# New prices for the clocks that choose a kernel's order of issue

## The chip, the cores and the metric

The kernel runs on one core of a Trainium2 chip. What is measured is the time of one execution in microseconds (us) on the device. Engines are called as in the profile: PE is the tensor engine's matmul and PEld its weight load, DVE the vector engine, ACT the scalar engine, POOL GpSimd, SP the queue that issues the transfers.

## The reference

One layer of a backbone over 256 latent tokens with 256 context tokens before them, width 2048, all in float32. Cut to what matters:

```python
h_ctx = rmsnorm(ctx) * (1 + scale_c) + shift_c      # scale, shift: products of silu(c) with w_mod
h     = rmsnorm(x)   * (1 + scale)   + shift
p     = h @ w_in                                    # 11552 columns, for both streams
r, k, v = split(conv3x3(p[rkv]))                    # the RWKV branch: 16 heads of 64
S = S*diag(w_t) + (S a_t) b_t^T + v_t k_t^T;  y_t = S r_t   # over the tokens, forwards and backwards
o = chunked_gla(q, k, v, g)                         # the GLA branch: 4 heads, forwards and backwards
mixed = sigmoid(g_a) * (y_a @ w_a) + sigmoid(g_b) * (y_b @ w_b)
out   = rmsnorm(x + gate * (mixed @ w_out))
```

The context is scanned first, and its last states are the first states of the latent tokens.

## The kernel before

Every product with a large weight is "dense": weights come in chunks of 512 KB (tile `raw`), ACT rounds half a chunk to a high part `wH`, DVE subtracts to get the rest `wL`, and PE sums three products of the parts (`three`). Dense work fills four stages in turn: the modulation and the first products; phase A (about 165 to 600 us in the profile), the rest of the columns for both streams with the GLA branch beside them; phase B (about 600 to 1170 us), columns that only latent tokens need, with the RWKV branch beside them; phase C, the two branch projections and the output projection.

The RWKV branch goes by eight pairs of heads. For each pair `fe_track` makes features on all engines, `gg_track` multiplies them in chunks, `inv_track` inverts the triangles on POOL in 30 steps of two instructions (`tm`, then `M`) between copies on ACT (`Lin`) and 32-wide transposes on DVE and two sets of small products on PE (`pH`, `pZ`), and `sc_track` carries the states through 8 chunk steps. A chunk step is a chain: product `p` on PE, copy `R` on ACT, product `pU`, copies into `UV` on DVE and ACT, product `pSs`, `Sn` on DVE, copies into `UV`, and the next `p`. In each of these products PE works on a part of its array (128x64 or 64x64 instead of 128x128); `pgl` has 64x128, `pH` and `pZ` 32x32.

The order is not written by hand. The program is cut into tracks (generators that yield an instruction, a list for one engine, or a claim to a bank of PSUM). While the program is built, `Issue.run` keeps a rough clock for each engine and advances the track whose next instruction can start first; among those of the same engine within 40 ns of it, the lowest priority number wins, and dense products have the highest number, 99. So dense work is what PE gets while nothing small is ready by the clocks. Each engine then runs its instructions in that fixed order on the chip, and waits at any whose inputs are late. The clocks decide nothing else: no instruction is added or left out by them.

The prices are in `Op.__init__` (line 31): for PE a weight load, a stream of columns and how many passes; for the others an offset and so many ns per element. `Issue.emit` (line 146) moves the clocks on:

```python
for _ in range(n):
    self.load_at = max(self.load_at, self.stream_at, there) + ld
    self.stream_at = max(self.load_at, e + 2)
    e = self.stream_at + stream
```

`there` is the time at which the inputs are there. Small float32 products that lie in different corners of the array are priced as running side by side (`corners`). `warm` (line 135) says whether PE has its full clock by the planner's own count, and doubles PE's prices where not; `cooling` (line 139) then prefers dense work. Two more uses of the prices: after 1200 ns of small work a dense list is taken if it stands in the same 40 ns (`since`), and `pace` (line 1491) lets gate columns start by how much small work was priced so far (`small`).

Every recorded operation has line 303 in the profile, where `Eng` calls the engine, so tiles tell them apart.

Of the kernel before, what the change touches and what calls it, by code (L numbers as in the profile page):

```python
# [24 lines left out]
class Op:  # L25
    """An instruction that a track wants issued."""

    __slots__ = ("key", "name", "call", "out", "ins", "cost", "table", "acc", "pe")

    def __init__(self, key, name, call, out, ins, func, acc, psum):  # L30
        self.key, self.name, self.call, self.out, self.ins, self.acc = key, name, call, out, ins, acc
        self.table = None if func not in TABLES else TABLES[func]
        n = 1
        for s in out.shape[1:]:
            n *= s
        per = 0
        if name in ("activation", "tensor_scalar", "scalar_tensor_tensor") and n > 1:
            per = sum(1 for x in ins if len(x.shape) == 2 and x.shape[1] == 1)
        if key == "pe":
            m = 1  # L40
            for s in ins[0].shape[1:]:
                m *= s
            if name == "transpose":
                m = n = ins[0].shape[0]
            two = ins[0].dtype == F32 and name != "transpose"
            self.pe = (2 if two else 1, m / 1.2, max(n, 64 if m > 32 else 32) * (2 if two else 1) / 2.4,
                       two and m <= 64 and (Issue.box(ins[0])[0], Issue.box(out)[0], m),
                       n * (2 if two else 1) * ins[0].shape[0] / 128)
            c = self.pe[0] * max(self.pe[1:3])
        elif key == "act":  # L50
            c = (51 if psum else 94) + 0.833 * n + 93 * per
        elif key == "dve":
            if name == "tensor_reduce":
                n = 1
                for s in ins[0].shape[1:]:
                    n *= s
            fast = name in ("tensor_copy", "tensor_scalar") and not psum
            c = (6 if name == "memset" else 68) + n * (0.521 if fast else 1.042) + 61 * per
        elif key == "pool":
            c = 35 + 0.83 * n if name == "memset" else 110 + 3.36 * n if name == "tensor_copy" else 149 + (  # L60
                1.667 if any(q == 0 and k > 1 for x in ins for q, k in x.ap[1:]) else 2.096) * n
        else:
            c = max(475.0, out.shape[0] * n * 4 / 360.0)
        self.cost = c

# [4 lines left out]
class Claim:  # L70
    """A free bank of PSUM from a group, once what is to be multiplied is there."""
# [5 lines left out]
class Issue:  # L77
    """Chooses the order in which the program is issued.

    Every engine runs its instructions in the order of issue. The program is cut into tracks: generators that yield  # L80
    an instruction (or a list of them for one engine), a claim to a bank of PSUM, or a condition. Of all tracks the
    one whose next instruction can start first, by rough clocks of the engines, is advanced; among those of one
    engine that could start at about the same time the one with the lowest priority number.
    """
# [3 lines left out]
    TICK, COLUMNS = 10240 / 3, 3060  # L88

    def __init__(self, ps, groups):  # L90
# [9 lines left out]
        self.corners, self.ticks = [], {}  # L100

# [20 lines left out]
    def start(self, ops):  # L122
        """When the inputs of some instructions are there."""
        w = 0.0
# [10 lines left out]
    def warm(self):  # L135
        """Whether the tensor engine has the full clock: the last tick of its monitor counted enough columns."""
        return self.ticks.get(int(self.t["pe"] // self.TICK) - 1, 0) >= self.COLUMNS

    def cooling(self):
        """Whether only products of the whole array now still bring the tick's count."""  # L140
# [5 lines left out]
    def emit(self, op):  # L146
        r = op.call()
        s = max(self.t[op.key], self.start([op]) + (1220 if op.key == "dma" else 0))
        if op.key == "pe":
# [4 lines left out]
            if corner and near and corner not in near and corner[2] == near[0][2] and len(near) < (4 if corner[2] == 32 else 2):  # L154
# [5 lines left out]
            there = self.start([op])  # L160
            for _ in range(n):
# [5 lines left out]
        else:  # L167
            e = s + op.cost
        if op.table is not None and op.table != self.table:
            self.table = op.table  # L170
            e += 1283.0
# [14 lines left out]
    def tile(self, pool, shape, dt, name, tag, bufs):  # L186
        """A tile of a rotating tag, with the time its slot falls free."""
# [7 lines left out]
    def keep(self, x):  # L195
        """A tile that lasts: its regions are written again as they are done with."""
# [30 lines left out]
    def step(self, tr, send):  # L227
        """Advances a track to its next wish."""
# [25 lines left out]
    def run(self, done):  # L254
        while not done():
# [9 lines left out]
            if best is None:  # L265
# [6 lines left out]
                if tr[6] == "pe" and self.since > 1200:  # L272
                    best = next((x for x in same if x[0] == 99), best)
                if tr[6] == "pe" and best[0] != 99 and 0.6 and self.cooling():
# [3 lines left out]
            if isinstance(g, list):  # L278
# [3 lines left out]
                if best[0] == 99:  # L282
                    self.since = 0.0
                else:
                    self.since += self.work - w0
# [24 lines left out]
class Pool:  # L310
    """A pool whose rotating tiles the clocks know."""
# [18 lines left out]
def hybrid_layer(tc, a, out):  # L330
    nc = tc.nc
    es = ExitStack()
    with es:
# [178 lines left out]
        def rsqrt(pool, v, shape, name):  # L512
            """1/sqrt(v): first guess from the exponent, then Newton steps."""
# [9 lines left out]
        def newton(v, y, t):  # L523
            """A step of y towards 1/sqrt(v)."""
# [11 lines left out]
        class Job:  # L536
            """chunks: (row tile, row tiles, first column, columns).

            take() claims what the job's result needs and says whether it could; a job that cannot start is passed
            over if it is marked so.  # L540
            """
# [10 lines left out]
        def pick():  # L552
            """The next weight chunk to fetch, or None."""
# [82 lines left out]
        def three(o, k, sw, H, L, xH, xL, first, last, **kw):  # L636
            """A product of two split operands; sw: the weights (H, L) are the moving ones."""
# [6 lines left out]
        def add_cm(src, c0, which, sl, prio, fn, take=None, skip=False, bank="acc"):  # L644
            """A column tile, channels on partitions; weights stationary."""
# [24 lines left out]
        def norm_track():  # L670
            """Both streams over their root mean square, channels on partitions."""
# [19 lines left out]
        def mod_track():  # L691
            """The shifts and scales, some row tiles' channels of each after the other."""
# [25 lines left out]
        def mod_cols(group, gv, w, b0, nk):  # L718
            """Sums over partitions, channels on partitions, with the bias."""
# [70 lines left out]
        def sz_track(acc, key):  # L790
            """2 * silu of a projected column tile (latent tokens)."""
# [46 lines left out]
        def gla_track(h, gp):  # L838
# [4 lines left out]
            def parts(src, name):  # L843
                """A transposed block as its high part and the rest."""
# [127 lines left out]
        def rows(p):  # L972
            """Where a pair's states and removals lie among the rows of the chunk products; the values lie in the other half."""
# [4 lines left out]
        def fe_track(p, fp, xp):  # L978
            """Per-token features of a head pair, channels on partitions."""
# [10 lines left out]
            def low_rank(o, i, d):  # L990
                """wH (xH + xL) + wL xH; the moving rows of direction d start with its high part in its own half."""
# [74 lines left out]
        def bv_track(p, xp, rc, rk):  # L1066
            """The bonus of the present token."""
# [23 lines left out]
        def bt_track(p, d, bk):  # L1091
            """What the states are updated by, tokens on partitions."""
# [10 lines left out]
        def gg_track(p, fp, xp):  # L1103
            """Chunk products."""
# [45 lines left out]
        def inv_track(p, fp, xp):  # L1150
            """Inverses of the unit triangles: diagonal blocks one matrix per lane, then the corner.

            A pair has half of the lanes: 32 per head, with 16 matrices of either block.
            """
# [49 lines left out]
        def aq_track(p, xp):  # L1204
            """What the states are multiplied with goes below the values' part of the chunk products."""
# [10 lines left out]
        def mv_track(p, fp, xp):  # L1216
            """Values with tokens on partitions."""
# [16 lines left out]
        def sc_track(p, xp):  # L1234
            """States through the chunks, both directions side by side; then group norm, bonus and gate."""
# [92 lines left out]
        # ================ issue ================  # L1328
        # first products: four column tiles side by side while the modulation is on its way
# [28 lines left out]
        # phase A: both streams  # L1358
        def low_track(acc, i):
            """A low-rank factor as (high part, rest) of each direction, one above the other."""  # L1360
# [80 lines left out]
        def gate_track():  # L1441
            """The last third of the modulation, by multiplying and adding."""
# [34 lines left out]
        # phase B: latent tokens only  # L1477
# [20 lines left out]
        # phase C: branch projections, merge, output projection  # L1498
# [63 lines left out]
        def out_track(n, i, acc):  # L1562
            """The gated residual of a column block, its squares, and its product with the last gain."""
# [38 lines left out]
        def lat_track():  # L1602
            """The latent tokens on their own, for when the context's are let go."""
# [113 lines left out]
        def tail_prep():  # L1717
            """The gate and the last norm's gain, over all partitions."""
# [64 lines left out]
```

## Time and profile before

| what | value |
|---|---|
| median of 3 runs | 1379.34 us (1372.85 to 1380.46) |
| span of the profiled execution | 1374.1 us; the page gives no other time of it, and the median lies 5.2 us above the span |
| busy: PE, DVE, ACT, POOL | 1285.3, 962.8, 717.2, 551.1 us |
| mean granted clock of PE | 0.980 of full speed |
| transfers | 220.40 MB, 160 GB/s over the span |

Busy time is a sum over instructions of one engine; PE's instructions overlap, and their ends are modelled, so what PE needs for one is read from the distance between two starts.

### The profile page before, as it was taken

What the parts mean: (1) busy time and instruction counts of PE and PEld (TensorE: products, weight loads), DVE (VectorE), ACT (ScalarE), POOL (GpSimd) and SP (SyncE); (2) the same over time, 40 slices, a digit from 0 to 9 for tenths busy, and PEclk for the clock granted to TensorE, in tenths of its full rate; (3) what the DMA queues carried; (4) which work ended last, traced back from release to release, by engine and by line L of the source; (5) the groups of instructions that cost most, each with busy time, mean ns of one, the idle gap of its engine ahead of it and who ended that gap; (6) DMA issues with size and microseconds to landing.
All of it is one profiled execution on the core that took longest, in us unless ns stands there. A gap on an engine that the chain in (4) does not pass through costs nothing.

```text
span 1374.1 us, 29066 instructions
## 1 busy us (share of the span) xinstructions
PE 1285.3 (94%) x11223; PEld 1070.4 (78%) x11223; DVE 962.8 (70%) x2013; ACT 717.2 (52%) x1449; POOL 551.1 (40%) x683
## 2 busy tenths in 40 slices
PE   5999999999999999998898989999999899999996
PEld 3555578788788898997787777877777788999876
DVE  4433496876965737776986878889868857668656
ACT  5222244443434534486485747686858556445443
POOL 0000466676570000005785567656857690000002
PEclk9999999999999999999999989999999999999999
DMA  9999465465462533665543424242433454589574
GB/s 347 339 334 316 132 194 177 137 178 162 146 186 84 140 95 107 172 174 150 139 118 90 112 67 120 78 120 78 113 93 82 104 152 131 163 242 276 181 245 141
DMA packets 311182, 220.40 MB, mean 160 GB/s; under 512 B 37354, under 2 KB 286724, under 8 KB 310532
## 3 DMA queue, kind: packets, MB, share of 16 engines
q1 hardware_dynamic: 311044, 218.55, 54.7%
q8 instruction: 88, 1.44, 0.4%
q14 instruction: 50, 0.41, 0.1%
HBM read 199.76 MB, written 12.46 MB: 154 GB/s over the span
## 4 chain that ended last, share of the span: by engine, by line
PE 56%; DVE 16%; POOL 11%; ACT 6%; issue 5%; DMA 5%; SPq 1%; DVEq 0%; ACTq 0%; POOLq 0%
PE acc L303 34%; PE pv L303 6%; DVE wL L303 5%; POOL M L303 5%; POOL tm L303 5%; PE pg L303 3%; ACT Lin L303 2%; DMA raw<-in_w_out_dram 2%; PE pgl L303 2%; PE pout L303 2%; ACT wH L303 1%; PE pS L303 1%; DVE kvo L303 1%; DVE UV L303 1%; PE pbt L303 1%
## 5 line engine op out<-in xcount | busy, mean ns | idle before, releaser
L303 DVE TENSOR_TENSOR wL<-raw,wH 128x512 fp32r<-128x512 f32 x484 | 379.0, 791 | 172.3 <-ACT wH L303 167.9
L303 ACT CAST wH<-raw 128x512 fp32r<-128x512 f32 x484 | 294.1, 615 | 323.9 <-PE acc L303 204.8
L303 PE MATMUL acc<-lH,wH 128*128 128x256 f32 x896 | 286.2, 319 | 0.5 <-ACT tg L303 0.5
L303 PE MATMUL acc<-lH,wL 128*128 128x256 f32 x896 | 255.7, 285 | 1.5 <-DVE wL L303 1.5
L303 PE MATMUL acc<-lL,wH 128*128 128x256 f32 x896 | 255.8, 286 | 0.0
L303 POOL TENSOR_TENSOR tm<-M 64x30 f32<-64x30 f32 (+14 forms) x240 | 166.2, 692 | 135.7 <-DVE M L303 117.9
L303 PEld LDWEIGHTS acc<-lH,wH 128*128 128x128 f32 x896 | 173.4, 194 | 26.0 <-issue 10.3
L303 POOL TENSOR_TENSOR M<-M,tm 64x30 f32<-64x30 f32 (+14 forms) x240 | 171.4, 714 | 18.7
L303 PEld LDWEIGHTS acc<-lL,wH 128*128 128x128 f32 x896 | 174.3, 195 | 2.0 <-issue 1.7
L303 PEld LDWEIGHTS acc<-lH,wL 128*128 128x128 f32 x896 | 173.7, 194 | 2.0 <-DVE wL L303 1.9
L303 PE MATMUL acc<-hH,wH 128*128 128x512 f32 (+1 forms) x416 | 168.6, 405 | 1.2 <-ACT lo L303 1.2
L303 PE MATMUL acc<-hH,wL 128*128 128x512 f32 (+1 forms) x416 | 157.8, 379 | 0.0
L303 PE MATMUL acc<-hL,wH 128*128 128x512 f32 (+1 forms) x416 | 156.9, 377 | 0.1
L303 PEld LDWEIGHTS acc<-hH,wH 128*128 128x128 f32 x416 | 78.8, 189 | 38.1 <-issue 22.9
L303 POOL TENSOR_TENSOR xs<-yg,fg 128x512 f32<-128x512 f32 (+1 forms) x10 | 13.5, 1367 | 217.5 <-DVE yg L303 217.5
L303 POOL TENSOR_TENSOR gw<-gw,csl 128x512 f32<-128x512 f32 x60 | 70.6, 1176 | 61.6 <-DMA gw<-in_w_mod_dram 61.4
L303 PEld LDWEIGHTS acc<-hH,wL 128*128 128x128 f32 x416 | 78.7, 189 | 15.4 <-DVE wL L303 0.4
L303 POOL TENSOR_TENSOR ga<-ga,gw 128x512 f32<-128x512 f32 x60 | 88.0, 1467 | 4.2
L303 PEld LDWEIGHTS acc<-hL,wH 128*128 128x128 f32 x416 | 79.0, 190 | 10.8 <-DVE hL L303 0.4
L303 PE MATMUL acc<-yH,wH 128*128 128x256 f32 x256 | 73.4, 287 | 0.7 <-DVE mt L303 0.7
L303 PE MATMUL acc<-yL,wH 128*128 128x256 f32 x256 | 72.0, 281 | 0.0
L303 PE MATMUL acc<-yH,wL 128*128 128x256 f32 x256 | 72.0, 281 | 0.0
(313 smaller groups left out, 2628.7 us busy)
## 6 DMA issues: line engine op xcount, KB each, us to landing
raw<-in_w_in_dram SPq DMA_DIRECT2D x174, 512.0 KB, 3.9
wm<-in_w_mod_dram SPq DMA_DIRECT2D x64, 512.0 KB, 7.0
gw<-in_w_mod_dram SPq DMA_DIRECT2D x64, 256.0 KB, 4.0
raw<-in_w_out_dram SPq DMA_DIRECT2D x32, 512.0 KB, 4.4
raw<-in_w_b_dram SPq DMA_DIRECT2D x16, 512.0 KB, 4.1
raw<-in_w_a_dram SPq DMA_DIRECT2D x16, 512.0 KB, 4.9
kv<-kvo SPq DMA_DIRECT2D x16, 256.0 KB, 3.7
tg<-tg SPq DMA_DIRECT2D x32, 128.0 KB, 2.9
```

The source lines that it names most:

```text
L303: op = Op("dma" if name == "dma_start" else self.key, name, lambda: f(*a, **k), aps[0], aps[1:], func, k.get("accum_out"), any(x.tensor.na ...
```

## The change

Only the planner's prices change. The instructions of every track stay the same, and so do priorities and buffers. PE: 13 ns more for each weight load, streams at 2.24 instead of 2.4 columns per ns, a delay of 100 ns at each change of the array's shape, and a wider rule for products that run side by side. ACT: 17 ns more from PSUM, twice the time per element for strided copies on 32 partitions. DVE: the scan at 2.18 ns per element instead of 1.042, no fast copy for strided ones on 32 partitions. DVE and POOL: 30% of an instruction's price on top, as far as the other one is busy. DMA: 340 instead of 360 bytes per ns. The planner's limit for "warm" falls. A rule with `BLOCK` is added that can't act while `BLOCK` is 0.0. Docstrings and comments are dropped.

```diff
-            self.pe = (2 if two else 1, m / 1.2, max(n, 64 if m > 32 else 32) * (2 if two else 1) / 2.4,
-                       two and m <= 64 and (Issue.box(ins[0])[0], Issue.box(out)[0], m),
+            self.shape = tuple(32 if x <= 32 else 64 if x <= 64 else 128 for x in (ins[0].shape[0], m))
+            self.pe = (2 if two else 1, 13 + m / 1.2, max(n, 64 if m > 32 else 32) * (2 if two else 1) / 2.24,
+                       two and min(m, ins[0].shape[0]) <= 64 and (Issue.box(ins[0])[0], Issue.box(out)[0], ins[0].shape[0], m),
...
-            c = (51 if psum else 94) + 0.833 * n + 93 * per
+            c = (68 if psum else 94) + 0.833 * n * (1 + strided(out, ins)) + 93 * per
...
-            c = (6 if name == "memset" else 68) + n * (0.521 if fast else 1.042) + 61 * per
+            fast = fast and not strided(out, ins)
+            c = (6 if name == "memset" else 68) + n * (0.521 if fast else 2.18 if "scan" in name else 1.042) + 61 * per
...
-            c = max(475.0, out.shape[0] * n * 4 / 360.0)
+            c = max(475.0, out.shape[0] * n * 4 / 340.0)
...
+def strided(out, ins):
+    return out.shape[0] == 32 and any(x.ap[-1][0] > 1 for x in (out, *ins) if len(x.ap) > 1)
...
-    TICK, COLUMNS = 10240 / 3, 3060
+    DRAIN = 100.0
+    BLOCK = 0.0
+    SHARE = 0.3
+    TICK, COLUMNS = 10240 / 3, 2000
...
-            if corner and near and corner not in near and corner[2] == near[0][2] and len(near) < (4 if corner[2] == 32 else 2):
+            if (corner and near and corner not in near and corner[2:] == near[0][2:]
+                    and len(near) < (128 // corner[2] if corner[2] >= 32 else 1) * max(1, 128 // corner[3])):
...
             there = self.start([op])
+            if op.shape != self.shape:
+                there = max(there, e + self.DRAIN)
+                self.shape = op.shape
...
             e = s + op.cost
+            if op.key in ("dve", "pool") and not any(x.tensor.name in self.psum for x in op.ins) and op.name != "memset":
+                o = "pool" if op.key == "dve" else "dve"
+                e += self.SHARE * min(op.cost, max(0.0, self.t[o] - s))
...
+                if tr[6] == "pe" and best[0] != 99 and 0 < self.dense < self.BLOCK:
+                    best = next((x for w, x in c if x[0] == 99 and isinstance(x[3], list) and w <= max(w0, self.t["pe"]) + 60), best)
```

## Rows read from the trace of the kernel before

**Rows 1.** Busy time of each engine (instructions), granted clock and DMA, by stage.

```profile
0.00:165.00 165.00, 146.89 (x1003) 82.89 (x1004) 65.40 (x195) 51.20 (x91) 12.92 (x26) 0.99 0.93 299
165.00:600.00 435.00, 420.88 (x2755) 364.61 (x2753) 308.60 (x624) 190.29 (x370) 169.38 (x139) 1.00 0.51 150
600.00:1170.00 570.00, 525.66 (x6041) 447.21 (x6042) 453.76 (x932) 380.94 (x801) 355.27 (x509) 0.96 0.43 112
1170.00:1374.10 204.10, 191.88 (x1428) 175.74 (x1428) 135.02 (x263) 94.73 (x187) 13.51 (x10) 0.99 0.67 207
```

**Rows 2.** The page's chain that ended last, by engine.

```profile
PE 56%; DVE 16%; POOL 11%; ACT 6%; issue 5%; DMA 5%; SPq 1%; DVEq 0%; ACTq 0%; POOLq 0%
```

**Rows 3.** What PE waited for, 600 to 1170 us: us in total, times, longest.

```profile
PE p L303 <- DVE UV L303: 8.9, 15, 1.7
PE pH L303 <- DVE Lin L303: 8.8, 5, 3.4
PE pbt L303 <- DVE bk L303: 4.1, 4, 1.9
...
PE pZ L303 <- DVE Lin L303: 1.7, 2, 1.3
```

**Rows 4.** What PE waited for, 165 to 600 us.

```profile
PE pT L303 <- DVE on L303: 4.3, 2, 2.7
...
PE pk L303 <- DVE ks L303: 3.1, 3, 1.3
```

**Rows 5.** Timeline of PE around a small product: start, us, instruction.

```profile
900.12 0.28 PE L303 MATMUL acc<-lH,wL 128*128 128x256 f32 x1
900.33 0.45 PE L303 MATMUL pU<-R,Z 64*64 64x64 f32 x8
...
901.05 0.28 PE L303 MATMUL acc<-lH,wL 128*128 128x256 f32 x1
901.17 0.28 PE L303 MATMUL acc<-lH,wH 128*128 128x256 f32 x1
```

**Rows 6.** Timeline of two engines later: a copy and the product that needs it.

```profile
907.57 0.24 ACT L303 COPY R<-p 128x128 f32<-128x128 f32 x1
...
908.09 0.45 PE L303 MATMUL pU<-R,Z 64*64 64x64 f32 x8
```

**Rows 7.** Groups of POOL, 600 to 1170 us: busy us, mean ns, idle before.

```profile
L303 POOL TENSOR_TENSOR M<-M,tm 64x30 f32<-64x30 f32 (+14 forms) x240 | 171.4, 714 | 18.7
L303 POOL TENSOR_TENSOR tm<-M 64x30 f32<-64x30 f32 (+14 forms) x240 | 166.2, 692 | 135.7 <-DVE M L303 117.9
```

**Rows 8.** A group of ACT in the same stretch.

```profile
L303 ACT COPY Lin<-GM 32x512 f32<-32x512 f32 x32 | 35.2, 1100 | 0.5
```

**Rows 9.** Groups of DVE in the same stretch.

```profile
L303 DVE TENSOR_TENSOR wL<-raw,wH 128x512 fp32r<-128x512 f32 x167 | 131.8, 795 | 17.7 <-ACT wH L303 17.0
...
L303 DVE COPY UV<-Sn 64x128 f32<-64x128 f32 x53 | 23.8, 449 | 1.0
L303 DVE TENSOR_TENSOR_SCAN C<-rmask,tw 128x512 f32<-128x512 bf16 x16 | 22.5, 1406 | 0.3
L303 DVE COPY UV<-pU 64x128 f32<-64x128 f32 x60 | 17.6, 293 | 13.9 <-PE pU L303 10.1 <-ACT UV L303 2.4
```

**Rows 10.** The same subtraction, 440 to 560 us.

```profile
L303 DVE TENSOR_TENSOR wL<-raw,wH 128x512 fp32r<-128x512 f32 x46 | 31.8, 690 | 26.6 <-ACT wH L303 25.9
```

**Rows 11.** Busy time by engine in the middle of that stretch, columns as in Rows 1.

```profile
480.00:520.00 40.00, 40.00 (x282) 35.74 (x282) 16.49 (x32) 14.51 (x29) 0.00 (x0) 1.00 0.34 93
```

**Rows 12.** Timeline of PE at the second pair's inverse.

```profile
745.48 1.92 PE L303 MATMUL pH<-Lin,GMo 32*32 32x32 f32 x64 [3.38 <-DVE Lin L303]
...
748.56 0.41 PE L303 MATMUL acc<-lH,wL 128*128 128x256 f32 x1
748.77 0.41 PE L303 MATMUL acc<-lH,wH 128*128 128x256 f32 x1
```

**Rows 13.** Busy time and granted clock there, columns as in Rows 1.

```profile
744.00:752.00 8.00, 6.52 (x97) 6.12 (x98) 5.57 (x10) 1.25 (x3) 0.00 (x0) 0.57 0.00 0
```

More of the change, by code (lines that the diff above doesn't have):

```diff
@@ L25 @@
 class Op:
-    __slots__ = ("key", "name", "call", "out", "ins", "cost", "table", "acc", "pe")
+    __slots__ = ("key", "name", "call", "out", "ins", "cost", "table", "acc", "pe", "shape")
     def __init__(self, key, name, call, out, ins, func, acc, psum):
@@ L100, in __init__ @@
         self.corners, self.ticks = [], {}
+        self.shape, self.dense = None, 0.0
     @staticmethod
@@ L283, in run @@
                     self.since = 0.0
+                    self.dense += self.work - w0
                 else:
+                    if best[6] == "pe":
+                        self.dense = 0.0
                     self.since += self.work - w0
```

## The prediction

> **What bounds the kernel now.** I read first the busy times by stage. The reader is to see that PE is busy for 92% of phase B and 97% of phase A [rows 1], so PE sets the pace, and order can win only what PE loses: 14.1 us idle in phase A (435 - 420.88), 44.3 us in phase B (570 - 525.66), 18.1 us in the first stage and 12.2 us at the end. Second, the chain that ended last: only 56% of it is PE, 27% is DVE and POOL [rows 2], so inputs made there are what PE's losses hang on. Third, what PE waited for: in phase B the chunk steps (`p` for `UV`), the inverse (`pH`, `pZ` for `Lin`) and the transposes `pbt` [rows 3]; in phase A `pT` and `pk` [rows 4]. [...]
>
> **The change part by part.** Nothing is added or removed on the chip. Each part is worth what the new order does to the waits.
>
> *PE, dense.* Before, the planner steps 106.7 + 2 = 108.7 ns from one dense product of 256 columns to the next; after, 13 + 106.7 = 119.7 ns. The trace shows 120 [rows 5]. So this price goes from 9% short to right. By itself this changes no PE work; it takes some 11 ns of unspoken reserve per product from inputs that other engines are making.
>
> *PE, small.* Take `pU`, four products of two passes. The old loop, followed by hand with loads and streams of 53.3 ns and 20 ns for each second corner, gives 0.38 us more than without it. In the trace the third dense product after the one at 900.12 starts at 901.05, against 900.48 at 0.12 us each: 0.57 us [rows 5]. The new loop has loads of 66.3, streams of 57.1, and 100 ns at both ends, behind which the load starts: 0.73 us. The error goes from 0.19 short to 0.16 long.
>
> *Side by side.* The lists of the chunk steps, of `pgc` and of `pH` and `pZ` hold only two different corners before one comes again and the count starts anew, so neither the old limit nor the new one is reached; `pgl` (64x128) has one corner per list; the products with w_mod have four under both. I take nothing.
>
> *Inverse.* Per pair the 30 steps come to 4960 elements for `tm` and as many for `M`: 60 x 149 + 4960 x (1.667 + 2.096) = 27.6 us by the old price. The trace has (171.4 + 166.2) / 8 = 42.2 us [rows 7]. With 30% on top, if DVE is always priced busy, 35.9 us. The four copies `Lin` go from 0.52 to 0.95 us each, where the trace has 1.10 [rows 8]. What the planner misses falls from 14.6 + 2.3 = 16.9 us to 6.3 + 0.6 = 6.9 us, by 59%. If the waits for the inverse shrink alike, 0.59 x (8.8 + 1.7) [rows 3] = 6.2 us are won; at the ends nothing or 10.5.
>
> *Scans.* `C` goes from 601 to 1184 ns, and the trace has 1406 [rows 9]: 72% of the error goes. Scans lie ahead of `bk` and `ks`; 0.72 x (4.1 + 3.1) [rows 3, 4] = 5.2 us. Ends: nothing and 7.2. `pT`'s 4.3 us wait behind a chain of one-column instructions whose price stays: nothing.
>
> *DVE and POOL.* The subtraction `wL` takes 690 ns [rows 10] where POOL does nothing [rows 11] and 795 ns in phase B [rows 9], where POOL is busy for 355/570 = 62%: 105 / 0.62 = 169 ns when both work, 0.28 of the old price of 601. So 0.3 is about right as a mean. It is already in the inverse above; on the chunk steps it reaches only a part, since the copy `UV<-Sn` takes 449 ns [rows 9] and is priced 135, then at most 175. I take nothing more.
>
> [...]
>
> [...]
>
> *Lost reserve.* Eight pairs by eight steps by three products are 192 places where a small product stands behind a chain. Against real time the planner's PE is now 0.16 us late per excursion instead of 0.19 early, so fewer dense products stand ahead of the next link. Where there is slack this is free: `R` ends at 907.81 and `pU` starts at 908.09 [rows 6], 0.28 us. `p` has none (8.9 us of waits in 15 cases [rows 3]). A product that waits stops all behind it on PE, the dense ones too. The ends are nothing and 192 x 0.16 = 31 us; the row of slack lies near the first, so I take 0.02 us a place, 4 us.
>
> *At nothing:* 17 ns on ACT copies from PSUM (less than the slack above); 340 bytes per ns, because transfers take 43% of the engines' time in phase B and the first stage's order of loads is fixed [rows 1]; `pace` and `since`, since gate columns that move from phase B to phase C are the same PE work there, where PE is busy for 94% [rows 1]. Without that cover every column tile moved would cost 16 x 3 x 0.12 = 5.8 us.
>
> The sum: 6.2 + 5.2 + 6 - 4 = 13 us less. The profile has a span of 1374.1 and gives no time around it; the median lies 5.2 above, and I carry that over: 1374.1 - 13 + 5.2 = 1366 us.
>
> **The rivals.** *Slower: the reserve decides.* The mechanism is the overpriced small product: PE reaches the chain's links earlier than planned and waits. For it speaks that DVE is busy for 80% of phase B [rows 1] and that `p` has no slack; against it the 0.28 us at `pU`. From 0.13 us a place on, (17.4 + 6.9) / 192, the kernel is slower by more than 0.5%; at 0.16 us it is 1379.3 - 17.4 + 31 = 1393 us.
>
> *No change.* The prices move all engines' clocks up together (DVE's 0.28, POOL's 30%, PE's 10% and more), order depends on their ratios, and waits turn up elsewhere as they go; or single instructions are held up by far more than the mean, such as the copy `UV<-Sn` with 449 ns against 293 for `UV<-pU` of the same size [rows 9], and a mean price doesn't reach their waits. For it speaks that the waits are many and short [rows 3]. With a fifth of the forecast's gain, 3 us, it is 1376 us. [...]
>
> [...]
>
> **How the numbers follow.** Chances: the forecast of 1366 (by itself 1353 to 1372) 0.40, the larger gain 0.14, no change 0.23, slower 0.23. The three runs lie 0.55% apart, so 0.5% (6.9 us) is about what can be told from no change. Faster by over 0.5%: 0.54; within it 0.23; slower 0.23. The range goes from 1338, the larger gain, to 1391, where most of the slower case still lies; about 2 in 10 are outside.
>
> **What would show it.** Right: the instruction counts stay the same; PE's waits for `Lin` fall under 6 us, those of `pbt` and `pk` under 3 together; the clock of phase B rises to 0.97; phase B's idle falls under 38 us. The lost reserve would show as more time in `p`, `pU` and `pSs` waiting for `UV` and `R`. Wrong: chain waits over 25 us more, or more stretches at the lower clock than before. A span that moves while PE's idle time does not would mean that the number of excursions and shape changes moved, which I hold fixed.

## The result, and the profile after

The changed kernel takes 1464.03 us (median of 4 runs, 1455.75 to 1469.93), the kernel before 1377.41 us: a ratio of 1.0612, 95% interval 1.0576 to 1.0649. The forecast of 1366 us and its range to 1391 us were wrong, in direction too.

The profile's page first. The instruction counts are those of before; PE is busy for 1342.6 us instead of 1285.3 (time in which at least one of its instructions is under way), and idle for 1468.2 - 1342.6 = 125.6 instead of 88.8 us. So 57 us of the 94 us of span are the same PE instructions taking longer, and 37 us are more idle time.

```profile
span 1468.2 us, 29163 instructions
...
PE 1342.6 (91%) x11223; PEld 1116.7 (76%) x11223; DVE 957.6 (65%) x2013; ACT 718.6 (49%) x1449; POOL 538.5 (37%) x683
...
PEclk9999999999999999997969796989787989999998
...
PE 55%; POOL 15%; DVE 14%; DMA 6%; ACT 5%; issue 5%; SPq 1%; DVEq 0%; ACTq 0%; POOLq 0%
```

The row of the clock shows where: from the 19th slice on, PE's granted clock drops again and again. Busy times by stage, columns and bounds as in [rows 1]:

```profile
165.00:600.00 435.00, 414.59 (x2678) 357.66 (x2676) 296.50 (x617) 184.29 (x360) 156.08 (x130) 0.99 0.50 144
600.00:1170.00 570.00, 498.65 (x5291) 414.54 (x5291) 409.86 (x841) 339.82 (x711) 344.70 (x509) 0.85 0.34 87
```

In phase B the clock falls from 0.96 to 0.85. The records of the granted clock hold two values alone in both kernels, 1.0 and 0.5 of full speed, so 0.85 is about 0.15 x 570 / 0.5 = 171 us at the lower level; counted from the records it is 174 us, and 44 before. DVE, ACT and POOL are all less busy than before. The reader sees a stage in which every engine waits more.

Fixed bounds hide what moved, so the next rows cut at the RWKV chains themselves, from the first `pq` to the last `p` ("the chain stage" from here on). First the kernel before, then the changed one: chain stage and what follows it, and under them the same of instructions that touch `acc`, the most numerous of the dense ones, which are meant by "dense products" from here on.

```profile
592.00:1185.00 593.00, 548.62 (x6287) 466.57 (x6288) 464.16 (x956) 395.22 (x833) 355.27 (x509) 0.96 0.43 113
1185.00:1374.00 189.00, 176.88 (x1237) 162.85 (x1233) 127.93 (x244) 87.43 (x168) 13.51 (x10) 0.99 0.69 212
...
592.00:1185.00 593.00, 329.30 (x2101) 274.19 (x2100) 23.55 (x56) 16.93 (x43) 0.96 0.43 113
1185.00:1374.00 189.00, 85.42 (x708) 84.38 (x708) 12.51 (x30) 0.00 (x0) 0.99 0.69 212
```

```profile
592.00:1212.00 620.00, 547.41 (x5826) 455.36 (x5826) 438.75 (x917) 370.54 (x786) 344.70 (x509) 0.85 0.34 88
1212.00:1468.00 256.00, 243.64 (x1780) 229.58 (x1777) 159.75 (x291) 118.38 (x222) 13.50 (x10) 0.98 0.71 212
...
592.00:1212.00 620.00, 298.50 (x1640) 239.65 (x1638) 23.23 (x55) 13.43 (x34) 0.85 0.34 88
1212.00:1468.00 256.00, 150.54 (x1251) 149.50 (x1251) 13.39 (x32) 4.16 (x11) 0.98 0.71 212
```

The chain stage starts at the same time and does 460 dense products fewer, 55 us of work at 0.12 us each [rows 5]. It is nevertheless 27 us longer, and what follows does 543 more (1251 instead of 708; the other 80 or so had come from ahead of the chain stage) and is 67 us longer: 27 + 67 = 94 us, the whole difference. Taking dense work away from between the links did not make the chains faster at this lower clock. PE is busy in the chain stage for as long as before (547 and 549 us) although it does 55 us of work less: so nearly all of the 57 us of longer work arise here.

What PE waited for, 600 to 1170 us, first two lines of the kernel before that [rows 3] leave out, then the changed kernel:

```profile
PE pSs L303 <- DVE UV L303: 4.0, 5, 1.3
PE pU L303 <- ACT R L303: 3.1, 4, 1.2
```

```profile
PE pH L326 <- DVE Lin L326: 18.0, 5, 6.2
PE p L326 <- DVE UV L326: 15.3, 18, 2.6
PE pU L326 <- ACT R L326: 6.2, 8, 2.6
PE pSs L326 <- DVE UV L326: 5.5, 5, 1.7
PE pbt L326 <- DVE bk L326: 4.2, 3, 1.8
```

All of these but `pbt` wait longer than before, and most of all `pH` of the inverse, which I had expected to gain (18.0 instead of 8.8 us); `pZ`, 1.7 us before [rows 3], is not in the list any more. One place shows how a link comes late (timeline of three engines, shortened):

```profile
807.78 2.17 DVE L326 TENSOR_TENSOR ar<-kn,eC 128x512 f32<-128x512 f32 x2
...
808.84 0.33 PE L326 MATMUL pSs<-UV,BK 128*64 128x64 f32 x2
...
809.97 0.30 DVE L326 COPY UV<-pU 64x128 f32<-64x128 f32 x1
810.30 1.22 DVE L326 TENSOR_TENSOR ar<-rc,eC 128x256 f32<-128x256 f32 x2
810.33 0.39 PE L326 MATMUL pSs<-UV,BK 128*64 128x64 f32 x5 [1.16 <-DVE UV L326]
...
812.35 0.28 PE L326 MATMUL acc<-lH,wL 128*128 128x256 f32 x1
...
815.28 0.70 PE L326 MATMUL p<-UV,GM 128*64 128x64 f32 x8 [2.65 <-DVE UV L326]
...
817.39 0.41 PE L326 MATMUL acc<-lL,wH 128*128 128x256 f32 x1
817.60 0.41 PE L326 MATMUL acc<-lH,wL 128*128 128x256 f32 x1
```

DVE works on features of the next pair (`ar`) and reaches the copy into `UV` at 809.97. PE has come to `pSs` at 808.84, stops half-way through it for 1.16 us, and then for 2.65 us at the next `p`. After that dense products start 0.21 us apart; the granted clock is 0.50 from 815.5 to 818 us. PE was early, the link was late, and behind it the clock was low.

Counted from the records over all 64 chunk steps, the median time from the end of `R` to the start of `pU` fell from 0.51 to 0.08 us. That is the reserve of which the prediction speaks: the time by which a link is ready before PE comes to it.

### The profile page after: what moved, and what is told of

Same layout as the page of the kernel before. It is cut to its first block, busy times and chain, and to the rows that moved or that the text cites. A ratio compares the mean times of both kernels' runs of the same rounds, so it can differ in the third digit from the quotient of the medians.

```text
span 1468.2 us, 29163 instructions
## 1 busy us (share of the span) xinstructions
PE 1342.6 (91%) x11223; PEld 1116.7 (76%) x11223; DVE 957.6 (65%) x2013; ACT 718.6 (49%) x1449; POOL 538.5 (37%) x683
## 4 chain that ended last, share of the span: by engine, by line
PE 55%; POOL 15%; DVE 14%; DMA 6%; ACT 5%; issue 5%; SPq 1%; DVEq 0%; ACTq 0%; POOLq 0%
PE acc L326 32%; POOL M L326 7%; POOL tm L326 7%; PE pout L326 5%; PE pv L326 5%; DVE wL L326 4%; PE pg L326 2%; ACT Lin L326 2%; DVE kvo L326 1%; PE pgl L326 1%; DMA wm<-in_w_mod_dram 1%; ACT wH L326 1%; DVE Lin L326 1%; PE pS L326 1%; DMA raw<-in_w_a_dram 1%
## 5 line engine op out<-in xcount | busy, mean ns | idle before, releaser
L326 DVE TENSOR_TENSOR wL<-raw,wH 128x512 fp32r<-128x512 f32 x484 | 368.0, 767 | 221.3 <-ACT wH L326 212.6
L326 PE MATMUL acc<-lH,wH 128*128 128x256 f32 x896 | 300.9, 336 | 1.4 <-DVE sz L326 0.9
L326 PE MATMUL acc<-lL,wH 128*128 128x256 f32 x896 | 265.1, 296 | 0.0
L326 PE MATMUL acc<-lH,wL 128*128 128x256 f32 x896 | 264.7, 295 | 0.0
L326 POOL TENSOR_TENSOR tm<-M 64x30 f32<-64x30 f32 (+14 forms) x240 | 161.4, 672 | 182.0 <-DVE M L326 164.0
L326 PEld LDWEIGHTS acc<-lH,wH 128*128 128x128 f32 x896 | 181.6, 203 | 28.4 <-issue 9.9
L326 PEld LDWEIGHTS acc<-lL,wH 128*128 128x128 f32 x896 | 184.4, 206 | 3.0 <-issue 2.5
L326 PEld LDWEIGHTS acc<-lH,wL 128*128 128x128 f32 x896 | 183.5, 205 | 0.2
L326 POOL TENSOR_TENSOR M<-M,tm 64x30 f32<-64x30 f32 (+14 forms) x240 | 167.2, 697 | 18.6
L326 POOL TENSOR_TENSOR ga<-ga,gw 128x512 f32<-128x512 f32 x60 | 84.8, 1413 | 4.2
```

Of the source, the lines that this page charges most:

```text
L326: op = Op("dma" if name == "dma_start" else self.key, name, lambda: f(*a, **k), aps[0], aps[1:], func, k.get("accum_out"), any(x.tensor.na ...
```

## The experiments

Three theories. A: PE's new prices do it, by taking the reserve and the dense work from between the links. B: the lower limit for "warm" hides from the planner that PE's granted clock falls. C: the prices of the other engines move the links. Two quantities are counted from the records: "long gaps" are the distances over 0.6 us between starts of PE products in the chain stage, less 0.3 us each, summed (39 us before, 73 after; the part of them ahead of `p`, `pU` and `pSs` is 17 and 34 us, ahead of `pH` 9 and 22); "excursions" are the places in it where a small product follows a dense one (258 before, 253 after). A time for which no number of runs is given is one run. The kernel before spread from 1371.76 to 1382.81 us in seven runs, so differences under some 11 us between single runs tell nothing. How long the clock stood at its lower level is counted from the records of the granted clock: in the chain stage 44 us before and 191 us after, in 7 and 16 stretches.

**PE's prices undone** (e1), in the changed kernel.

```diff
-            self.pe = (2 if two else 1, 13 + m / 1.2, max(n, 64 if m > 32 else 32) * (2 if two else 1) / 2.24,
+            self.pe = (2 if two else 1, m / 1.2, max(n, 64 if m > 32 else 32) * (2 if two else 1) / 2.4,
...
-    DRAIN = 100.0
+    DRAIN = 0.0
```

> The changed kernel with the three new prices of PE undone (no 13 ns per load, 2.4 columns per ns, no delay for the array's shape); the other new prices and the lower limit for 'warm' stay. Theory A (PE's prices thin out the dense work between the links of the chains, so the clock falls): back at or under the time before, 1360 to 1385 us, mean granted clock 0.97 or more. Theory B (the lower limit hides from the planner that PE cools): still slow, over 1420 us, clock under 0.95. Theory C (the prices of DVE, ACT, POOL and DMA move the chains' links to where PE waits): still slow, over 1420 us, with PE's waits of phase B as in the changed kernel.

1410.26 us beside 1376.37 of the kernel before, clock 0.951, long gaps 33 us. So 54 of the 87 us go with three numbers, and the gaps are back under those of before. But 34 us stay, and the time lies between the theories' ranges. The chain stage still has 102 us at the lower level of the clock, so the time there does not follow from long gaps alone. Not everything is undone: with `DRAIN` at 0 the line stays by which a load of another shape starts behind the end of the stream before, and by the planner's loop an excursion to `pU` costs 0.45 us, where the kernel before has 0.38.

**PE's prices and the limit alone** (e2), in the kernel before.

> The kernel before with PE's three new prices and the lower limit for 'warm' alone; the prices of DVE, ACT, POOL and DMA and the rule for products side by side as before. Theory A: slow, 1430 to 1490 us, clock 0.94 or less, fewer than 1500 dense products between 600 and 1170 us. Theory C: as before, 1365 to 1390 us. Theory B: slow too, since it has the lower limit; the two are told apart by the kernel with that limit alone.

1509.67 us, clock 0.923, 1479 dense products in the chain stage (1365 between 600 and 1170 us), long gaps 81 us: over theory A's range and slower than the whole change, 133 us above the kernel before. The other new prices, taken together, soften what PE's do. C is out as the main cause.

**A stronger guard** (e3), in the changed kernel.

```diff
-        return 3100 - self.ticks.get(k, 0) > ((k + 1) * self.TICK - t) * rate
+        return 4500 - self.ticks.get(k, 0) > ((k + 1) * self.TICK - t) * rate
```

> The changed kernel with one number of the planner's guard against cooling raised (3100 to 4500), so that dense work is taken before small work more often in phase B; every price as in the changed kernel. If the loss is the clock (theory A's second half): time falls to 1390 to 1430 us and the clock rises to 0.96 or more. If the loss is the waits of PE for links that come late: the time stays at 1450 us or more although the clock rises, since the chains get later still.

1460.21 us at a clock of 0.957, as expected of waits. Its chain stage:

```profile
598.00:1293.00 695.00, 619.21 (x6543) 522.04 (x6543) 482.46 (x986) 410.58 (x858) 350.07 (x509) 0.93 0.39 106
...
598.00:1293.00 695.00, 386.56 (x2355) 318.04 (x2355) 26.95 (x64) 17.57 (x45) 0.93 0.39 106
```

717 dense products more than in the changed kernel, a better clock, and no time won: idle time is as high (695 - 619 = 76 us), long gaps are 73 us, and there are 317 excursions. Forcing dense work ahead of small products makes the chains later and does not make their links ready. What the low clock costs by itself this run can't tell: 64 excursions more at up to 0.57 us (36 us, an estimate from [rows 5]) stand against the 89 us less at the lower level.

**The other engines' prices alone** (e4), in the kernel before.

> The kernel before with the new prices of DVE, ACT, POOL and DMA alone (scan, strided copies, 17 ns from PSUM, 30% when DVE and POOL are both busy, 340 bytes per ns); PE's prices and the limit for 'warm' as before. Theory A: at or under the time before, 1340 to 1385 us, clock 0.98. Theory C: slow, over 1420 us.

1394.67 us, clock 0.957, long gaps 28 us: neither theory's range. Long gaps in the chain stage do fall, but it starts at 619 instead of 592 us: something is lost ahead of it.

**The limit alone** (e5), in the kernel before.

```diff
-    TICK, COLUMNS = 10240 / 3, 3060
+    TICK, COLUMNS = 10240 / 3, 2000
```

> The kernel before with only the planner's limit for 'warm' lowered as in the change. Theory B (the lower limit hides from the planner that PE cools): slow, over 1420 us, clock under 0.95. Theories A (PE's prices) and C (the other engines' prices): as before, 1365 to 1390 us.

1396.48 us beside 1379.73: 17 us, above A's range and far below B's. The chain stage has the counts of before (2100 dense products, 258 excursions, 597 us); 14 us are lost ahead of it, as it starts at 606 instead of 592 us. The wider rule for products side by side was never undone alone. Between e4 and e1 stand that rule, the limit and what is left of the delay, 16 us together; the limit alone has 17, which leaves no visible cost for the rule.

**An excursion at its measured price** (e6), in the changed kernel.

```diff
-    DRAIN = 100.0
+    DRAIN = 20.0
```

> The changed kernel with 20 instead of 100 ns for a change of the array's shape, by which an excursion to pU is priced 0.57 us, as the trace of before has it, instead of 0.73. If the overprice of 0.16 us was the harm: 1370 to 1400 us and no more than 45 us of long gaps (over 0.6 us) on PE in the chain stage. If it is the lost reserve (a right price leaves none, and the price of before was 0.19 us short): still over 1425 us, long gaps over 55 us.

1446.02 us, long gaps 54 us (expected: over 55). An accurate price gives back only 18 us, so most of the harm was not that 0.73 us is too long. The median from `R` to `pU` is 0.14 us: a right price leaves little reserve.

**A reserve of another kind** (e7): all prices of the change stay, and results are said to come 150 ns later.

```diff
-    LAT = {"pe": 200.0, "act": 135.0, "dve": 135.0, "pool": 135.0, "dma": 920.0}
+    LAT = {"pe": 350.0, "act": 285.0, "dve": 285.0, "pool": 285.0, "dma": 920.0}
```

> The changed kernel with 150 ns more in the planner for the time from any engine's end to the use of its result (PE 350 instead of 200, ACT, DVE and POOL 285 instead of 135); all prices stay. This gives the plan a reserve in another way. Lost reserve: long gaps of the chain stage fall from 73 to under 50 us and the time to 1390 to 1435 us, with more dense products between the links. If dear small work does the harm by other ways (the rule that breaks small work after 1200 ns, the pace of the gate columns): 1450 us or more.

1419.66 us, 44 us less than the changed kernel; long gaps 53 us (expected: under 50), clock 0.958, median from `R` to `pU` 0.42 us. Its chain stage, with more dense products between the links (2055 instead of 1638) at about the same length:

```profile
588.00:1218.00 630.00, 574.71 (x6241) 484.36 (x6241) 461.88 (x951) 393.04 (x829) 344.50 (x509) 0.92 0.39 104
...
588.00:1218.00 630.00, 343.52 (x2057) 281.91 (x2055) 22.71 (x54) 16.80 (x43) 0.92 0.39 104
```

No price of PE was touched, and half of the 87 us is back: dear small work does not need to be made cheaper for that, a reserve is enough. The other half stays, with 106 us at the lower level of the clock in the chain stage.

**PE cheaper still** (e8). In the kernel before, loads and streams times 0.92.

> The kernel before with PE's loads and streams priced 8% lower still, further from what the trace shows. If a reserve helps without end: fewer long gaps than before's 39 us and 1355 to 1377 us. If the kernel before stands near the best reserve: 1377 to 1410 us, with fewer long gaps but chains that end later.

1379.41 us beside 1379.73, long gaps 35 us, clock 0.969. The chain stage ends later, as expected (1220 instead of 1185 us). Prices still further below the trace cut the gaps a little and bring no time.

**The 30% between DVE and POOL alone** (e9), in the kernel before.

```diff
             e = s + op.cost
+            if op.key in ("dve", "pool") and not any(x.tensor.name in self.psum for x in op.ins) and op.name != "memset":
+                o = "pool" if op.key == "dve" else "dve"
+                e += self.SHARE * min(op.cost, max(0.0, self.t[o] - s))
```

> The kernel before with one new price alone: DVE and POOL instructions cost up to 30% more while the other engine is busy. Lost reserve: this price makes links later in the plan, so more dense products stand between them: fewer long gaps on PE in the chain stage than the 39 us of before, no more low clock than before's 44 us there, 1345 to 1377 us. If theory C (vector prices move links to where PE waits) holds for this part: 1385 us or more.

1363.19 us (4 runs, 1357.28 to 1364.97) beside 1379.01: ratio 0.9888, 95% interval 0.9838 to 0.9937. This kernel beats both, and lies in the range of the lost reserve. Long gaps are 28 us; its chain stage, and what PE waited for there:

```profile
595.00:1199.00 604.00, 572.07 (x6529) 490.12 (x6529) 485.12 (x987) 406.61 (x853) 362.67 (x509) 0.97 0.45 122
1199.00:1360.00 161.00, 148.70 (x997) 134.86 (x995) 110.32 (x214) 74.97 (x148) 13.52 (x10) 0.99 0.65 208
...
595.00:1199.00 604.00, 360.52 (x2343) 304.21 (x2341) 27.66 (x66) 16.81 (x43) 0.97 0.45 122
```

```profile
PE pU L307 <- ACT R L307: 3.7, 3, 2.4
...
PE pH L307 <- DVE Lin L307: 2.8, 3, 1.8
...
PE p L307 <- DVE UV L307: 2.5, 10, 0.6
```

241 dense products more than before, 29 us of work at 0.12 us each, fit into a chain stage that is 11 us longer, `pH` waits 2.8 instead of 8.8 us [rows 3] and `p` 2.5 instead of 8.9. Less is left for the end, 161 instead of 189 us. The chain stage has 38 us at the lower level, 44 before.

**The same with the stronger guard** (e10, 4500).

> The same kernel with the planner's guard against cooling raised from 3100 to 4500. If the guard costs only what it adds in excursions (as in e3_guard, with 64 more of them): slower than e9_share_alone by 5 to 20 us at a higher clock. If low clock is what is left to win: faster than e9_share_alone by 5 us or more.

1377.57 us, at a lower clock (0.973 against 0.979), with 271 excursions instead of 263: slower by 14 us, as expected, though not at a higher clock.

**Half of PE's prices at a time**, in the changed kernel: first without the 13 ns and 2.24 (e11), then without the delay of 100 ns (e12).

> The changed kernel with 13 ns per load and 2.24 columns per ns undone, and the delay of 100 ns for the array's shape kept. Theory A with lost reserve, by shares of the price: the dense price falls from 119.7 to 108.7 ns, an excursion from 0.73 to 0.6 us or less; between e1_no_pe_prices (1410 us) and the changed kernel (1464): 1415 to 1450 us. If the delay alone did the harm: over 1455 us. If the dense price alone did it: 1400 to 1415 us.

> The changed kernel without the delay for the array's shape; 13 ns per load and 2.24 columns per ns kept. With 20 ns it was 1446 us. By shares: 1425 to 1445 us. If the delay alone did the harm: 1400 to 1415 us.

1426.65 and 1422.83 us, long gaps 57 and 52 us. The first lies in its range, the second just under its own. Each half alone gives back 37 to 41 us, both 54. Neither did the harm alone. The planner's loop prices an excursion at 0.65 us in the first, where the expectation says 0.6 or less, and at 0.53 in the second, where the load still waits for the end of the stream before.

**What hurt in the other engines' prices**: e9's kernel with one more of them each, first the rate of transfers (e13), then the scan (e14), then the copies (e15).

> The kernel of e9_share_alone with transfers priced at 340 instead of 360 bytes per ns. If the DMA rate does e4's harm: 1380 to 1400 us, and the first product of the chain stage starts 10 us or more later than in e9_share_alone (595 us). If not: 1355 to 1370 us.

> The kernel of e9_share_alone with the scan at 2.18 ns per element. If a truer price of the scan saves the waits behind it (my prediction: 5 us): 1352 to 1365 us. If it does e4's harm: 1380 us or more.

> The kernel of e9_share_alone with the new prices of copies (17 ns more from PSUM, strided copies on 32 partitions). If they help the inverse (my prediction: part of 6 us): 1352 to 1365 us. If they do e4's harm: 1380 us or more.

1390.23, 1364.76 and 1371.79 us beside the 1363.19 of e9. The rate of transfers costs 27 us; the copies cost 9, which is inside the spread of single runs and in neither expected range; the scan costs and wins nothing that shows. With the rate the chain stage starts at 605 us, 9 us later than in e9, and the loss begins early: here is the stretch from 80 to 150 us, first of e9's kernel, then with the rate, with what PE waited for there (in e9's kernel nothing is listed).

```profile
80.00:150.00 70.00, 70.00 (x466) 40.36 (x465) 27.95 (x72) 19.20 (x36) 0.00 (x0) 1.00 0.86 274
```

```profile
80.00:150.00 70.00, 62.68 (x433) 33.51 (x431) 21.33 (x56) 16.06 (x31) 0.00 (x0) 0.92 0.81 261
...
PE pg L307 <- DMA wm<-in_w_mod_dram: 2.7, 3, 1.7
```

PE loses 7 us there that it had not lost, and 33 instructions; 2.7 of the 7 us are waits for loads of `wm`. Most of the rest of the 27 us is in the chain stage:

```profile
605.00:1224.00 619.00, 586.88 (x6496) 502.57 (x6494) 477.22 (x983) 405.05 (x849) 361.31 (x509) 0.93 0.44 118
```

Beside e9's chain stage this shows the clock nearly alone. PE is idle for the same 32 us (619 - 587 and 604 - 572) and does 25 dense products fewer, but 85 us are at the lower level instead of 38, and PE is busy for 15 us longer. With 3 us for the missing products that is 18 us for 47 us, 0.4 us for each. The same count against e9 has 9 us for 37 in e15 and 7 us for 34 in e4, 0.2 for each.

## Why the prediction was wrong

**What bounds the kernel** agrees with the result, and the plan's arithmetic was right: dense 119.7 ns, an excursion from 0.38 to 0.73 us where the chip takes 0.57.

**Lost reserve** is the step that failed, and with it the sum's third term, 6 us won at the clock. It took 0.02 us at each of 192 places, 4 us, because one row showed 0.28 us of slack [rows 6]. Long gaps ahead of `p`, `pU` and `pSs` rose from 17 to 34 us, which is 0.09 us a place, 17.6 us: inside its ends of 0 and 0.16, and over four times what was taken. The slack that the row showed was itself made by the old, too short prices: the median of all 64 chunk steps fell from 0.51 to 0.08 us once they were raised. In its sum the prediction took the price of an excursion alone; the 9% by which each of some eight dense products ahead of a link (2100 / 258) was underpriced, which it had called unspoken reserve, belonged to the same reserve and got no term. And it counted places of the chunk steps alone: the products of the inverse stand behind a chain too, and the long gaps ahead of `pH` rose from 9 to 22 us, where a gain of 6.2 was forecast. e6 and e7 bear this out: the measured excursion price brings back 18 us, a reserve put in elsewhere 44 us.

**The clock** had the wrong sign. The sum's 6 us was my guess, and no run shows it; the runs showed a loss in its place. Measured are 147 us more at the lower level in the chain stage (191 instead of 44). At 0.2 to 0.4 us for each, as e4, e13 and e15 have it beside e9, that is 30 to 60 us, an estimate, and so may be most of the 57 us by which PE is busy longer. In both kernels the low stretches stand behind waits. Of the chain stage's stretches, 7 of 7 before and 15 of 16 after begin inside a distance of over 1 us between two starts of PE products, or less than 4 us behind one, where 22% and 31% of all moments of the stage lie so. The rival "slower" had the mechanism of the waits and came to 1393 us, because it priced a wait once: that dense products behind one started 0.21 instead of 0.12 us apart [rows 5, 12] is not in its sum. Why the clock fell as far as it did stays open in part: e1 has no more long gaps than the kernel before and still 102 us at the lower level. Nor does a run show the larger gain, from which the range's lower end of 1338 us comes: the fastest kernel of all, e9's, took 1363.19 us.

Of the prediction's own signs of being wrong, more stretches at the lower clock came (16 instead of 7 in the chain stage); the waits for `Lin`, which were to fall under 6 us, rose to 18.

**At nothing** was wrong twice. The rate of 340 bytes per ns costs 27 us (e13), added to e9's kernel; a fixed order of loads does not fix when the planner believes them landed, and so how it orders PE among them (in e13 PE's order departs from e9's within the first 26 us). The limit for "warm" costs 17 us (e5), and no term of the sum stands for it.

**DVE and POOL, inverse**: alone, the price of 30% does what was forecast (e9). `pH` waits 6.0 us less and `pZ` 1.5, where I had 6.2 for both with the copies' price beside it. The whole gain is 16 us; `p` waits 6.4 us less for `UV` from DVE too (1.6 more for `UV` from ACT), for which I had taken nothing. In the whole change this gain is buried: there `pH` waits longer. So a price that is right only as a mean did shorten a wait. What it is the mean of lies far apart: of the 484 `wL` of the kernel before, the 125 with POOL beside them for over 90% of their time have a median of 1002 ns and reach 1808, and the 286 with POOL beside them for under 2% reach 696 at most. The 169 ns of the prediction were the mean over such cases.

**Scans**: 5.2 us expected; in the changed kernel `pbt` and `pk` wait 4.2 and 3.3 us against 4.1 and 3.1 [rows 3, 4], so none of it came. e14 does not settle what the scan's price is worth alone: it stands on e9's kernel, where these two waits had already fallen to 0.4 and 1.3 us (0.3 and 0.7 in e14).

**Dense work that moves to phase C is the same work**: right as far as it went (543 products, 67 us later on), but I had no term for a chain stage that does less and still takes longer.

Added up, mostly from single runs, 54 (PE's prices) + 17 (limit) + 27 (transfers) + 9 (copies) + 2 (scan) - 16 (DVE and POOL) = 93 us beside the 87 measured. That the sum comes out does not make these the sizes of the parts: each was taken on another kernel, and PE's prices with the limit cost 133 us without the others (e2) and not 54 + 17. Open stay why the limit and the rate of transfers cost what they do ahead of the chain stage, and why the clock is low where links are not late.

## What to carry to other kernels

A planner's price that is wrong on the busiest engine can be load-bearing: with PE priced too short, most links were ready before PE came to them (a median of 0.51 us ahead, and 0.08 with PE's true prices). Before making such a price true, count the slack that it leaves at all links, not at one, and put the reserve somewhere explicit. Filler between the links of a chain is cheap only in time that the chain needs anyhow: 241 dense products more cost 11 us in e9, where links came late less often, and 717 more cost 75 us in e3, where they were forced ahead of the links. So watch how much filler a stage does and what is left behind it, not only how long the stage is. And change one price at a time: one of this change's prices was worth 1.1% alone and was buried under the others.

## What the runs showed of the hardware

Dense products of 256 columns start 0.12 us apart at full clock [rows 5] and 0.21 us apart at the lower level [rows 12] (medians of 120 and 213 ns over 3308 and 62 distances in the kernel before), so that their distance alone tells which level holds in a row of the timeline. An excursion from dense products (128x128) to one group of 64x64 products (eight records of `pU`) costs 0.57 us, with 0.38 us from the group's first start to the next dense start; these are the medians of the 48 such places at full clock in the kernel before, one of which is in [rows 5]. The subtraction `wL` was slower in phase B after the change too: 818 ns there against 690 in the kernel before where POOL does nothing [rows 10, 11].

```profile
L326 DVE TENSOR_TENSOR wL<-raw,wH 128x512 fp32r<-128x512 f32 x123 | 99.6, 818 | 22.7 <-ACT wH L326 21.6 <-PE p L326 0.6
```
